# Moving an on-chip tile from a 32-byte offset to a multiple of 128 bytes

## The chip, the cores and the metric

The kernel runs on one core of a Trainium2 chip. The metric is the device time of one execution in microseconds; the median of the runs shown is compared.

## The reference

Two layers of a decoder trunk on 256 tokens of width 1024, all in float32. Each layer is a half-step feed-forward block, a token mixer and a second half-step feed-forward block, each on an RMS-normalised input. What matters here is the product of that normalised input with wide weight matrices:

```python
for l in range(DEPTH):
    h = h + 0.5 * swiglu(rms_norm(h, ffn1_norm[l]), ffn1_w_in[l], ffn1_w_out[l])
    u = rms_norm(h, mix_norm[l])
    (z_s, xbc, dt_s, qkv, z_d, b_d, a_d, gate_s, gate_d) = jnp.split(u @ w_in[l], split_points, axis=-1)
    y_s = mamba2_branch(z_s, xbc, dt_s, ...)      # state-space branch
    y_d = deltanet_branch(qkv, z_d, b_d, a_d, ...)  # gated delta rule branch
    merged = (jax.nn.sigmoid(gate_s) * (y_s @ ssm_w_branch[l])
              + jax.nn.sigmoid(gate_d) * (y_d @ dn_w_branch[l]))
    h = h + merged @ w_out[l]
    h = h + 0.5 * swiglu(rms_norm(h, ffn2_norm[l]), ffn2_w_in[l], ffn2_w_out[l])
return rms_norm(h, final_norm)
```

swiglu(x) is (silu(gate) * up) @ w_out with gate and up from x @ w_in (1024 to 2 x 2816).

## The kernel before

The weights stream from HBM in halves of 512 KB, in the order in which they are used: tile `wraw` takes a half, ScalarE rounds it to `whi`, VectorE writes the rest to `wlo` (lines 93 to 104). Every product of two float32 matrices is three matmuls of rounded parts: high by high, high by low, low by high. Five raw and five split halves are in flight.

`norm_in` makes the input of each sub-layer: per token tile of 128 tokens the norm, four transposes a half (`hnT`, in PSUM), then ScalarE writes the high part into `uTh` and VectorE the low part into `uTl`. Both are [128 partitions, 8 k tiles, 256 tokens], 8192 bytes a partition. They are read in two ways:

- `tok_chunk` (products named `t` and `f`) loads a 128 x 128 piece of uTh or uTl into TensorE and streams 512 columns of the weights past it (lines 209 to 211).
- `chan_chunk` (products named `fc`, `kk`, `qq`, `vv`, `zd`, `bc`, `xs`) loads a 128 x 128 piece of the weights and streams 256 columns, the tokens, of uTh or uTl past it (lines 214 to 216). `psm` does the same with 48 weight columns.

The products `o` (the second feed-forward matrix and the mixer's output) and `b` (the branches) have the form of `t`, but load the tiles gh, gl, mh, ml, bh or bl, which other pools hold.

In a feed-forward block `f` comes first, then 20 chunks of `fc`, then `o`. In the mixer the steps of the table ORDER follow each other: projections, the triangular inverse, the recurrence, the state-space products (`stb`, `ydb`, `yob`, which wait for the decay mask `dc`), gates and branches. The order on each engine is that in which the code issues its instructions, with the norm chains moved up by a priority.

Tiles of a pool with one buffer lie one behind the other in each partition, in the order of their first use, each padded to 32 bytes. In the pool `cpool` the order is h, cs, mhalf, one, Y0, Y1, uTh, uTl, nw, lp, rp, wsh, wsl; the pools of the weights and of everything else follow. `mhalf` is a column of 4 bytes, the exponent of the power that POOL takes for each norm. `lp` holds the parameters of the convolutions (LPW = 257 columns), `nw` the norm's weights, Y0 and Y1 are scratch of the inverse.

Of the kernel before, what the change touches and what calls it, by code (L numbers as in the profile page):

```python
# [7 lines left out]
F32 = mybir.dt.float32  # L8
# [8 lines left out]
P = 128  # L17
# [12 lines left out]
NRAW = 5  # L30
NSPL = 5
START = 2
# Steps of the token mixer in issue order; the weight stream follows it (see _layout).
# s decay scalars, M decay masks, z/k/q/v/d/b/x projections (gate of group, delta rule k q v and gate,
# state-space B C and x), K/Q/V what follows a projection, I triangular inverse, R recurrence,
# P state-space products of B and C, D decay, S/T state-space output, g branch gates,
# o/y first operand of the branches, N delta rule branch.
ORDER = """
z20 s z10 z11 s z21 s M k1 k0 q1 k2 k3 K1 K0 q3 q0 K3 K2 v0 q2 I Q0 I Q3 I z30 v1 z31 Q2 v2 V0 I v3
V1 I V3 I Q1 V2 d0 R R R b3 R b2 b0 R b1 R d2 R x00 R d1 x01 R d3 R R P R g100 g101 D0 S0 x10 T0 D1  # L40
# [5 lines left out]
def trunk_kernel(ctx, tc, x, wst, wsm, norms, lpar, rpar, cst, out):  # L46
# [38 lines left out]
    def small(shape, name, bufs=2):  # L85
        return sm.tile(shape, F32, tag=name, name=name, bufs=bufs)

# [1 line left out]
    n_halves = 2 * wst.shape[0]  # L89
    state = {"loaded": 0, "prepped": 0, "taken": 0, "last": None, "hold": False}  # L90
    raws, halves = {}, {}
# [32 lines left out]
            nc.sync.dma_start(nw[:], norms[i].partition_broadcast(P))  # L124
        return [nw[:, n * 512 : (n + 1) * 512] for n in range(2)]

# [1 line left out]
    h = cpool.tile([P, 2, D], F32, name="h")  # L128
    cs = cpool.tile([P, CW], F32, name="cs")
    row = slots.tile([1, D], F32, tag="y0", name="row")  # L130
# [14 lines left out]
    LIMT = cs[:, 3 * P + 64 : 4 * P]  # L145
    SEL = [cs[:, 4 * P : 5 * P], cs[:, 5 * P : 6 * P]]
    LAST = cs[:, 6 * P : 7 * P]
    mhalf = cpool.tile([P, 1], F32, name="mhalf")
    V.memset(mhalf[:], -0.5)

    one = cpool.tile([1, P], F32, name="one")
# [9 lines left out]
    uTl = cpool.tile([P, KT, S], F32R, name="uTl")  # L161

    def rstd_of(t):
        """1 / sqrt(mean(h^2) + eps) of one token tile"""
        ss = small([P, 2], "ss")
        for n in range(2):
            junk = tmp2("junk")
            act(junk[:], h[:, t, n * 512 : (n + 1) * 512], AF.Square, scale=1.0 / 32.0, accum_out=ss[:, n : n + 1])
        z = small([P, 2], "zz")
        ts(z[:, 0:1], ss[:, 0:1], ss[:, 1:2], ALU.add, EPS, ALU.add)  # L170
        rsqrt(z[:, 1:2], z[:, 0:1], [P, 1])
        return z[:, 1:2]
# [16 lines left out]
        return ins, done  # L189

    def norm_in(nw, add=None):
        """residual update (add) and the normalised, transposed, split input of the next sub-layer"""
        for t in range(2):
            with tc.high_priority(offset=PRI):
                if add:
                    add(t)
                ins, done = rms_chain(t, nw)
            if t == 0:
                state["hold"] = False
                n = state["taken"]  # L200
                if not add:
                    ahead("prepped", n + 1, prep)
                    with tc.issue_after(done[0].ins), tc.issue_after(done[1].ins):
                        ahead("prepped", n + START, prep)
                with tc.issue_after(ins.ins):
                    ahead("prepped", n + 2, prep)
# [9 lines left out]
        PE.matmul(ps, wl, mh, start=False, stop=stop)  # L216

    def tok_chunk(ps, ks):
        """512 output columns for both token tiles, contracted over the k tiles ks, two to a half"""
        ws = [(k, take()) for k in ks[::2]]  # L220
        for t in range(2):
            for k0, (wh, wl) in ws:
                for k in range(2):
                    kt = k0 + k
                    mm3(
                        ps[t][:],
                        uTh[:, kt, t * P : (t + 1) * P],
                        uTl[:, kt, t * P : (t + 1) * P],
                        wh[:, k * 512 : (k + 1) * 512],
                        wl[:, k * 512 : (k + 1) * 512],  # L230
                        kt == 0,
                        kt == KT - 1,
                    )

    def chan_chunk(ps):
        """256 output channels, channel-major: two halves of four k tiles."""
        ws = [take(), take()]
        for a in range(2):
            for q in range(2):
                wh, wl = ws[q]  # L240
                for k in range(4):
                    kt = 4 * q + k
                    c0 = k * 256 + a * P
                    mm3w(
                        ps[:, a * 256 : (a + 1) * 256],
                        wh[:, c0 : c0 + P],
                        wl[:, c0 : c0 + P],
                        uTh[:, kt, :],
                        uTl[:, kt, :],
                        kt == 0,  # L250
                        kt == KT - 1,
                    )

    def out_chunks(ps, stat, ks, last, group=1, split=False):
        """[k tile, 1024] halves accumulated in ps[t][n]; stat(kt, t) -> (hi, lo)."""
        for g0 in range(0, len(ks), group):
            kk = ks[g0 : g0 + group]
            ws = [(k, take()) for k in kk]
            for t in range(2):
                order = [(k, n) for n in range(2) for k in range(len(kk))]  # L260
                if t == 1 and not split:
                    order = [(k, n) for k in range(len(kk)) for n in range(2)]
                for k, n in order:
                    k, (wh, wl) = ws[k]
                    sh, sl = stat(k, t)
                    mm3(
                        ps[t][n][:], sh, sl,
                        wh[:, n * 512 : (n + 1) * 512], wl[:, n * 512 : (n + 1) * 512],
                        k == 0, k == last,
                    )  # L270

    def close(po, stat, n_k, nw):
        """last weights token tile by token tile, then the residual and the next norm"""
        out_chunks(po, stat, list(range(2)), n_k - 1, group=2)
        out_chunks(po, stat, list(range(2, n_k - NSPL)), n_k - 1)
        state["hold"] = True
        out_chunks(po, stat, list(range(n_k - NSPL, n_k)), n_k - 1, group=NSPL, split=nw is None)

        def add(t):
            for n in range(2):  # L280
                hv = h[:, t, n * 512 : (n + 1) * 512]
                stt(hv, po[t][n][:], 0.5, hv, ALU.mult, ALU.add)

        if nw is None:
            return add
        norm_in(nw, add)

# [1 line left out]
    def ffn(nxt):  # L289
        gh = [slots.tile([P, 8, S], F32R, tag=t_, name="gh") for t_ in ("sA", "sB", "sC")]  # L290
        gl = [slots.tile([P, 8, S], F32R, tag=t_, name="gl") for t_ in ("sD", "sE", "sF")]
# [34 lines left out]

        return close(po, stat, 22, nxt)

# [1 line left out]
    def mixer(l, nxt):  # L330
        with tc.issue_after(state["last"].ins):
            lp = cpool.tile([P, LPW], F32, tag="lp", name="lp")
            nc.sync.dma_start(lp[:], lpar[l])
            rp = cpool.tile([P, RPW], F32, tag="rp", name="rp")
            nc.sync.dma_start(rp[:], rpar[l].partition_broadcast(P))
            wsr = s2.tile([P, KT, 48], F32, tag="s2", name="wsr")
            nc.sync.dma_start(wsr[:], wsm[l])
# [11 lines left out]
        open_ = {}  # L349

        def tok_unit(key, part, done):
            """part 0 or 1 of the contraction, or all of it at once"""
            if part != 1:
                open_[key] = [accb("t0"), accb("t1")]
            tok_chunk(open_[key], range(KT) if part is None else range(4 * part, 4 * part + 4))
# [7 lines left out]
            tok_unit(("z", g), part, lambda t, ps: act(yz[g][:, t, :], ps[:], AF.Silu))  # L363

        def conv(ps, ti, dest, bias):
            """causal depthwise convolution and SiLU of one channel tile"""
            cp = lp[:, 5 * ti : 5 * ti + 5]
            ca = s2.tile([P, S], F32, tag="ca", name="ca", bufs=2)
            if bias:
# [6 lines left out]

        z_unit(0, None)

# [1 line left out]
        la = small([P, 2, 40], "la", 1)  # L380
        sp = small([P, 2, 40], "sp", 1)
        ac = small([P, 2, 40], "ac", 1)
# [59 lines left out]
        Gp = pq[:, 0]  # L442
        Bp = pq[:, 1]

# [1 line left out]
        kP = slots.tile([P, 4, 4, 2, 64], F32, tag="sA", name="kP")  # L446
        qP = slots.tile([P, 4, 4, 2, 64], F32, tag="sB", name="qP")
        Q = slots.tile([P, 16, P], F32, tag="sC", name="Q")
# [17 lines left out]
        oe = small([P, 4, 4], "oe", 1)  # L466

        def masks():
            """masked decay factors of all pairs, natural (dN) and transposed (dT)"""
            for hp in range(4):  # L470
                gb = s2.tile([P, 2, 4, 64], F32, tag="s2", name="gb")
                nc.sync.dma_start(
# [25 lines left out]
            act(eG[:], Gp, AF.Exp)  # L498

        def turned(src, hp):  # L500
            """token-major copy (in PSUM) and its squared norms"""
            bank = trb("turned")
            for c in range(4):
                PE.transpose(bank[:, c * P : (c + 1) * P], src[:, hp, c].rearrange("p a i -> p (a i)"), ident)
# [5 lines left out]
            return bank, nb  # L510

        def own(bank, x, y, hp):
            """x^T y of each head with itself, chunk by chunk"""
            for c in range(4):
                for a in range(2):
                    PE.matmul(
# [69 lines left out]
            return rest()  # L586

        def invert():
            """(I + Q)^-1: 16-blocks by substitution, one block to a partition, then doubling"""
            dq1 = dram.tile([P, 16, 16], F32, tag="dq1", name="dq1")  # L590
            dq2 = dram.tile([P, 2, 16, 16], F32, tag="dq2", name="dq2")
            for b in range(8):
# [151 lines left out]
            for _ in g:  # L744
                pass

# [1 line left out]
        def zd_unit(hp):  # L748
            ps = accb("zd")
            chan_chunk(ps)  # L750
# [138 lines left out]
            v = tg[s_][:, :, n * 512 : (n + 1) * 512]  # L889
            tok_unit(("g", s_, n), part, lambda t, ps: act(v[:, t, :], ps[:], AF.Tanh, scale=0.5))  # L890

# [1 line left out]
        brT = {}  # L893

        def dn_T(hp):
# [149 lines left out]
def _layout(inp):  # L1045
# [2 lines left out]
    f32 = np.float32  # L1048

    def cols(w):  # L1050
        """[K, 512*n] -> token-major units [128, 4 k tiles, 512], two per 512 columns"""
        n = w.shape[1] // 512
        a = w.reshape(2, 4, P, n, 512)
        return a.transpose(3, 0, 2, 1, 4).reshape(2 * n, P, 2048)

    def chans(w):
        """[1024, 256*n] -> channel-major units [128, 8 k tiles, 256]"""
        n = w.shape[1] // 256
        return w.reshape(8, P, n, 256).transpose(2, 1, 0, 3).reshape(n, P, 2048)

    def rows(w):
        """[256*n, 1024] -> units [128, 2 k tiles, 1024]"""
        n = w.shape[0] // 256
        return w.reshape(n, 2, P, 1024).transpose(0, 2, 1, 3).reshape(n, P, 2048)

# [96 lines left out]
```

## Time and profile before

| | |
|---|---|
| median of 3 runs | 1604.63 us (1603.78 to 1605.13) |
| profiled execution, first to last instruction | 1604.1 us; it lists no time of its own beside this span |
| granted TensorE clock | 0.997 |
| TensorE busy | 1581.0 us, 99% |
| VectorE busy | 1069.5 us, 67% |
| ScalarE busy | 885.3 us, 55% |
| HBM read | 280.94 MB |

A row of a group ends with its count, then its busy time and the mean of one in ns, then idle time before it. PE rows are matmuls, PEld rows the loading of the operand that stays in the array, which overlaps. A row of the timeline begins with the start and the duration in us. A row of the windows view begins with the stretch and its length, then busy time and count of PE, PEld, DVE, ACT and POOL (only those that have any), and ends with the granted clock, the share of the DMA engines and GB/s.

### The profile page before, as it was taken

To read this page: it belongs to the slowest core of one execution; us is meant where nothing else is said; L and a number is where in the kernel's file an instruction comes from. 1 tells how busy PE (TensorE), PEld (TensorE's weight loads), DVE (VectorE), ACT (ScalarE), POOL (GpSimd) and SP (SyncE) were. 2 spreads that over 40 slices of the span, in tenths; PEclk is the share of its full clock that TensorE was granted. 3 is DMA by queue.
4 is the path that set the end of the run, shared out by engine and by line. 5 is a ranking of instruction groups with operands and counts; after the bars stand their busy time and mean duration, and the time that the engine had idled before them with its cause. 6 is when DMAs were issued, how large, how long until landed. Compare 5 with 4: busy or idle time off the path is not lost.

```text
span 1604.1 us, 28895 instructions
## 1 busy us (share of the span) xinstructions
PE 1581.0 (99%) x11696; PEld 1425.3 (89%) x11696; DVE 1069.5 (67%) x1546; ACT 885.3 (55%) x1418; POOL 66.5 (4%) x60
## 2 busy tenths in 40 slices
PE   8999999999999999999999999999999999999998
PEld 7999879999888888999899987899998888889986
DVE  5555568957899666555465555699578986665554
ACT  5454467765575554444454445676756665454443
POOL 0000020000010000000000002010000100000000
PEclk9999999999999999999999999999999999999999
DMA  7555565543555455555465665556345455555562
GB/s 267 192 188 193 164 207 177 184 140 119 185 197 170 147 169 191 190 185 192 163 211 189 191 196 181 174 186 185 111 139 191 171 173 168 172 171 186 190 200 95
DMA packets 91915, 284.73 MB, mean 178 GB/s; under 512 B 22069, under 2 KB 23045, under 8 KB 90758
## 3 DMA queue, kind: packets, MB, share of 16 engines
q1 hardware_dynamic: 91782, 282.90, 54.2%
q8 instruction: 91, 1.49, 0.4%
q14 instruction: 42, 0.34, 0.1%
HBM read 280.94 MB, written 1.92 MB: 176 GB/s over the span
## 4 chain that ended last, share of the span: by engine, by line
PE 89%; DVE 4%; DMA 2%; ACT 2%; POOL 1%; issue 1%; SPq 0%; POOLq 0%; ACTq 0%; DVEq 0%
PE fc L214 9%; PE fc L216 9%; PE fc L215 9%; PE o L211 6%; PE o L210 5%; PE o L209 5%; PE t L209 3%; PE t L210 3%; PE t L211 3%; PE b L209 3%; PE b L210 3%; PE b L211 3%; PE xs L216 1%; PE xs L215 1%; PE xs L214 1%; DMA dc<-rdram 1%
## 5 line engine op out<-in xcount | busy, mean ns | idle before, releaser
L63 DVE TENSOR_TENSOR wlo<-wraw,whi 128x1024 fp32r<-128x1024 f32 x504 | 613.7, 1224 | 382.2 <-ACT whi L60 374.9
L60 ACT ACTIVATE whi<-wraw 128x1024 fp32r<-128x1024 f32 x504 | 531.1, 1060 | 424.6 <-PE fc L215 176.2
L214 PE MATMUL fc<-uTh,whi 128*128 128x256 f32 x1280 | 357.4, 279 | 0.0
L215 PE MATMUL fc<-uTl,whi 128*128 128x256 f32 x1280 | 357.0, 279 | 0.0
L216 PE MATMUL fc<-uTh,wlo 128*128 128x256 f32 x1280 | 357.0, 279 | 0.0
L215 PEld LDWEIGHTS fc<-uTl,whi 128*128 128x128 f32 x1280 | 240.6, 188 | 0.2
L214 PEld LDWEIGHTS fc<-uTh,whi 128*128 128x128 f32 x1280 | 240.6, 188 | 0.2
L216 PEld LDWEIGHTS fc<-uTh,wlo 128*128 128x128 f32 x1280 | 240.6, 188 | 0.0
L209 PE MATMUL o<-whi,gh 128*128 128x512 f32 x352 | 137.3, 390 | 0.0
L210 PE MATMUL o<-wlo,gh 128*128 128x512 f32 x352 | 137.2, 390 | 0.0
L211 PE MATMUL o<-whi,gl 128*128 128x512 f32 x352 | 137.0, 389 | 0.0
L209 PE MATMUL t<-whi,uTh 128*128 128x512 f32 x256 | 103.3, 404 | 1.2 <-ACT uTh L60 1.2
L210 PE MATMUL t<-wlo,uTh 128*128 128x512 f32 x256 | 101.6, 397 | 0.0
L211 PE MATMUL t<-whi,uTl 128*128 128x512 f32 x256 | 101.1, 396 | 0.0
L209 PE MATMUL b<-whi,bh 128*128 128x512 f32 x192 | 77.2, 404 | 3.7 <-ACT bh L60 3.7
L211 PEld LDWEIGHTS o<-whi,gl 128*128 128x128 f32 x352 | 66.1, 188 | 13.6
L210 PEld LDWEIGHTS o<-wlo,gh 128*128 128x128 f32 x352 | 66.1, 188 | 13.5
L209 PEld LDWEIGHTS o<-whi,gh 128*128 128x128 f32 x352 | 66.1, 188 | 13.5
L210 PE MATMUL b<-wlo,bh 128*128 128x512 f32 x192 | 75.9, 395 | 0.0
L211 PE MATMUL b<-whi,bl 128*128 128x512 f32 x192 | 74.9, 399 | 0.0
L214 PE MATMUL xs<-uTh,whi 128*128 128x256 f32 x256 | 73.1, 286 | 0.0
L216 PE MATMUL xs<-uTh,wlo 128*128 128x256 f32 x256 | 71.8, 280 | 0.4 <-DVE wlo L63 0.4
(262 smaller groups left out, 2940.4 us busy)
## 6 DMA issues: line engine op xcount, KB each, us to landing
wraw<-in_wst_dram SPq DMA_DIRECT2D x504, 512.0 KB, 4.4
dc<-rdram SPq DMA_DIRECT2D x8, 1024.0 KB, 8.1
nw<-in_norms_dram SPq DMA_DIRECT2D x6, 512.0 KB, 5.8
gb<-rdram SPq DMA_DIRECT2D x8, 256.0 KB, 6.1
h<-in_x_dram SPq DMA_DIRECT2D x4, 256.0 KB, 3.2
out_dram<-fo SPq DMA_DIRECT2D x4, 256.0 KB, 2.3
dq<-X SPq DMA_DIRECT2D x2, 256.0 KB, 4.7
cs<-in_cst_dram SPq DMA_DIRECT2D x1, 384.0 KB, 9.2
```

Of the source, the lines that this page charges most:

```text
L60: return A.activation(out=o, in_=i, func=func, **kw)
L63: return V.tensor_tensor(out=o, in0=a, in1=b, op=op)
L209: PE.matmul(ps, lh, rh, start=start, stop=False)
L210: PE.matmul(ps, lh, rl, start=False, stop=False)
L211: PE.matmul(ps, ll, rh, start=False, stop=stop)
L214: PE.matmul(ps, wh, mh, start=start, stop=False)
L215: PE.matmul(ps, wh, ml, start=False, stop=False)
L216: PE.matmul(ps, wl, mh, start=False, stop=stop)
```

## The change

`mhalf` is taken from the pool `sm`, at the far end of the partition, in place of `cpool`. With it gone, the tiles between it and rp move down by 32 bytes, and `lp` is declared 272 columns wide in place of 257, so that rp and everything behind it stay where they were. The transfer into lp still fills 257 columns. Comments are dropped, with empty lines in their place.

```diff
-    mhalf = cpool.tile([P, 1], F32, name="mhalf")
+    mhalf = sm.tile([P, 1], F32, name="mhalf", bufs=1)
...
-            lp = cpool.tile([P, LPW], F32, tag="lp", name="lp")
-            nc.sync.dma_start(lp[:], lpar[l])
+            lp = cpool.tile([P, 272], F32, tag="lp", name="lp")
+            nc.sync.dma_start(lp[:, 0:LPW], lpar[l])
```

No instruction is added, removed or moved on any engine. What changes is the start of these tiles within a partition (bytes, and the remainder by 128):

| tile | before | after |
|---|---|---|
| mhalf | 28288 (0) | 223872 (0) |
| one | 28320 (32) | 28288 (0) |
| Y0, Y1 | 28832, 30880 (32) | 28800, 30848 (0) |
| uTh | 32928 (32) | 32896 (0) |
| uTl | 41120 (32) | 41088 (0) |
| nw | 49312 (32) | 49280 (0) |
| lp | 53408 (32) | 53376 (0) |
| small tiles of `sm` (scalars, sums, la, sp, ac and others) | from 223872 on | each 32 further |

rp starts at 54464 (64) and wsh at 54912 (0) in both; the weight tiles, gh, gl, mh, ml, bh and bl start on multiples of 128 in both.

## The prediction

> **What bounds the kernel now.** I read the head of the page first, then the chain, then the groups of TensorE instructions, and then the times at which single matmuls start.
>
> ```profile
> span 1604.1 us, 28895 instructions
> PE 1581.0 (99%) x11696; PEld 1425.3 (89%) x11696; DVE 1069.5 (67%) x1546; ACT 885.3 (55%) x1418; POOL 66.5 (4%) x60
> PE 89%; DVE 4%; DMA 2%; ACT 2%; POOL 1%; issue 1%; SPq 0%; POOLq 0%; ACTq 0%; DVEq 0%
> ```
>
> TensorE is busy 99% of the span and holds 89% of the chain that ended last. So a matmul that becomes shorter counts nearly in full, and the question is only whether the addresses change a matmul. The groups give the counts by kind (lines 214 to 216 have the same count each, as have 209 to 211):
>
> ```profile
> L214 PE MATMUL fc<-uTh,whi 128*128 128x256 f32 x1280 | 357.4, 279 | 0.0
> L209 PE MATMUL o<-whi,gh 128*128 128x512 f32 x352 | 137.3, 390 | 0.0
> L209 PE MATMUL t<-whi,uTh 128*128 128x512 f32 x256 | 103.3, 404 | 1.2 <-ACT uTh L60 1.2
> L214 PE MATMUL xs<-uTh,whi 128*128 128x256 f32 x256 | 73.1, 286 | 0.0
> L214 PE MATMUL kk<-uTh,whi 128*128 128x256 f32 x128 | 35.9, 281 | 0.0
> L209 PE MATMUL f<-whi,uTh 128*128 128x512 f32 x64 | 26.4, 415 | 0.9 <-ACT uTh L60 0.9
> ```
>
> The first operand named is the one that streams, the second the one that is loaded. In the channel-major products (fc, xs, and kk, qq, vv, zd, bc with 128 a line each) uTh and uTl stream, 256 columns at a time: 3 x (1280 + 256 + 5 x 128) = 6528 matmuls. In the token-major ones (t, f) uTh and uTl are loaded and the weights stream, 512 columns: 3 x (256 + 64) = 960. The o products have the same form as t, but load gh and gl, which already start on a multiple of 128 bytes.
>
> The durations in these rows overlap (390 ns x 1056 is far more than the time that o takes), so they price nothing. I take the distance between starts instead: first and last row of an unbroken run in the timeline, and the count from a windows row cut to that tile.
>
> ```profile
> 31.34 0.28 PE L215 MATMUL fc<-uTl,whi 128*128 128x256 f32 x1
> 137.51 0.28 PE L216 MATMUL fc<-uTh,wlo 128*128 128x256 f32 x1
> 31.34:137.51 106.17, 106.17 (x912) 106.17 (x911) 7.87 (x19) 6.96 (x19) 1.00 0.59 190
> 137.63 0.39 PE L209 MATMUL o<-whi,gh 128*128 128x512 f32 x1
> 193.19 0.39 PE L211 MATMUL o<-whi,gl 128*128 128x512 f32 x1
> 137.62:193.20 55.58, 55.57 (x246) 46.00 (x246) 1.38 (x2) 0.00 (x0) 1.00 0.57 182
> 518.33 0.39 PE L210 MATMUL t<-wlo,uTh 128*128 128x512 f32 x1
> 534.66 0.39 PE L211 MATMUL t<-whi,uTl 128*128 128x512 f32 x1
> 518.32:534.67 16.35, 16.35 (x72) 13.15 (x70) 0.60 (x1) 1.00 0.51 165
> 217.32 0.28 PE L214 MATMUL psm<-uTh,wsh 128*48 128x256 f32 x1
> 219.99 0.28 PE L216 MATMUL psm<-uTh,wsl 128*48 128x256 f32 x1
> 217.31:220.00 2.69, 2.68 (x24) 2.68 (x23) 0.00 (x0) 1.00 1.03 337
> ```
>
> In the fc and t windows one of the counted matmuls began before the window. So fc: 106.17 us / 910 intervals = 116.67 ns. o: 55.56 / 245 = 226.8 ns. t: 16.33 / 70 = 233.3 ns. psm (uT streams, only 48 columns are loaded): 2.67 / 23 = 116 ns. The clock column reads 1.00 in all of them.
>
> This is the row that decides the sign. t and o stream the same weights tiles in the same 512 columns at the same clock; t loads from an address with remainder 32, o from one with remainder 0, and t takes 6.5 ns more for each matmul.
>
> **The change part by part.**
>
> *The loaded operand (t, f).* After the change uTh and uTl have remainder 0 as gh and gl have. I take the o spacing: 960 x 6.5 ns = 6.2 us. Nothing in the rows makes it a loss.
>
> *The streamed operand (6528 matmuls).* Before shows no 256-column stream from an aligned tile, so this is bounded. If a matmul costs a fixed part, not below zero, and a part per column, then 256 aligned columns cost at least half of 512 aligned ones: 226.8 / 2 = 113.4 ns, a gain of 3.3 ns. If only the loaded operand feels its address, they stay at 116.7: nothing. If the grid works the other way on a stream, by as much for each column as on the load (6.5 ns on 512 columns, so 3.3 on 256), they go to 120 ns, a loss of 3.3 ns. I take 113.4, because of a match: half of t's 233.3 is 116.67, exactly the fc spacing. Every matmul with one operand off the grid passes 2.19 columns per ns, whichever operand it is and however long the stream, and the only kind with both on the grid passes 2.26. psm says the same from another side: with 48 loaded columns in place of 128 the spacing stays at 116, so it is not the load's length that holds fc. So 6528 x 3.3 = 21.5 us. psm adds 48 x 3 ns = 0.1 us.
>
> By the Trainium skill, "TensorE: Matmul & The Clock Gate", section "Part 2: What happens when you issue a matmul", loading the next weights takes no read bandwidth from the running matmul, since there are two read ports. By that rule the address of a loaded operand could not lengthen a matmul that streams 512 columns; the 6.5 ns between t and o speak against it, and the sum by it would lose its first term.
>
> *What ScalarE and VectorE do with the moved tiles.*
>
> ```profile
> L60 ACT ACTIVATE uTh<-hnT 128x512 fp32r<-128x512 f32 x24 | 14.0, 595 | 12.8 <-PE hnT L184 11.6
> L60 ACT ACTIVATE tg<-t 128x512 f32<-128x512 f32 x16 | 9.5, 593 | 9.5 <-PE t L211 9.2
> L63 DVE TENSOR_TENSOR uTl<-hnT,uTh 128x512 fp32r<-128x512 f32 x24 | 15.7, 687 | 5.8 <-ACT uTh L60 5.7
> L63 DVE TENSOR_TENSOR ml<-mT,mh 128x512 fp32r<-128x512 f32 x8 | 5.5, 688 | 0.1
> ```
>
> Writes to the tiles that are off the grid take as long as those to tg and ml, which are on it. I cost nw, lp, Y0, Y1, one and the small tiles (which move by 32 bytes the other way) at nothing by the same rows. The wider lp moves no more data: its transfer still fills 257 columns. mhalf is read by POOL as before. One loaded operand goes off the grid, la, which eight matmuls (psr) load: 8 x 6.5 ns, 0.05 us.
>
> *What of the gain lies off the path.* In the mixer the chain leaves TensorE for a stretch:
>
> ```profile
> 407.49 1.22 DVE wlo L63
> 409.11 8.53 DMA dc<-rdram
> 428.39 2.29 DVE dc L63
> 437.22 1.10 PE stb L853 x2
> 407.00:485.00 78.00, 75.05 (x592) 65.30 (x589) 71.01 (x97) 50.51 (x74) 8.99 (x3) 0.98 0.56 192
> 407.00:485.00 78.00, 49.81 (x224) 36.53 (x224) 0.00 (x0) 0.00 (x0) 0.98 0.56 192
> 407.00:485.00 78.00, 35.05 (x112) 21.06 (x112) 0.00 (x0) 0.98 0.56 192
> ```
>
> The four chain rows show stb waiting for a mask that comes by DMA and VectorE; the window rows (all work, then uTh's, then uTl's instructions) show VectorE busy 71.0 of 78 us (third pair) and 224 + 112 = 336 of the matmuls in question. Five projections and two half gates stand there: 240 matmuls of 256 columns, 96 t. If they shrink, TensorE waits longer at stb and for the weight splits behind it. I give all of it up, in both layers: 480 x 3.3 + 192 x 6.5 = 2.8 us.
>
> At each of six norms the first token tile's matmuls cover the second tile's norm:
>
> ```profile
> 199.19 0.39 PE L209 MATMUL t<-whi,uTh 128*128 128x512 f32 x1
> 203.85 0.40 PE L211 MATMUL t<-whi,uTl 128*128 128x512 f32 x1
> 204.35 0.66 PE L184 MATMUL hnT<-cs,hn 128*128 128x128 f32 x4
> ```
>
> About 22 matmuls finish before the transposes hnT can begin, which wait on VectorE. Their gain becomes wait: 6 x 22 x 6.5 ns = 0.9 us.
>
> Sum: 6.2 + 21.5 + 0.1 - 2.8 - 0.9 = 24.1 us. The profiled span is 1604.1 us, 0.5 below the median of the runs, 1604.63; taken from the median it gives 1580.5 us.
>
> **The rivals.**
>
> *Only the loaded operand gains* (streams stay at 116.7). For it: the equal 116.67 may be the pace of something else that happens once a matmul. Against it: the match with t, and psm. Then 960 - 192 - 132 = 636 matmuls x 6.5 = 4.1 us: 1600.5.
>
> *Between the two*: streams at 114 to 116; 1584 to 1597.
>
> *Streams gain more than half of o.* The rows hold a pace for loading alone:
>
> ```profile
> 239.80 0.39 PE L494 MATMUL lb<-ac,cs 128*128 128x32 f32 x2
> 240.02 0.37 PE L214 MATMUL kk<-uTh,whi 128*128 128x256 f32 x1
> ```
>
> Two lb matmuls load 128 columns each and stream 32; they take 0.22 us, 110 ns each. At 110 the 6048 streams on the path would save 6.7 ns each: 40.5 + 4.1, so 1560. It needs most of o's 226.8 ns to be a cost that 256 columns do not bear.
>
> *Slower: two reads on one grid collide.* If a stream and a load whose remainders are equal meet in one bank, fc, whose operands are now 32 bytes apart, would go to the 120 ns of the bound above: 6528 x 3.3 = 21.5 us more, less 4.1 for the loads: 1622. It decides from 117.3 ns up (4.1 us / 6528 = 0.6 ns). Against it: t, whose operands are 32 bytes apart too, is slower than o, whose are not.
>
> *Nothing happens.* If t is slower than o for its loop (24 matmuls into one bank in a row, where o changes bank more often) and not for its address, all stays: 1604.6. In o three matmuls in a row go to one bank without a slow one among them, so I give it little. The Trainium skill, "SBUF — State Buffer", section "Door 1: The DMA port swizzle (why [64,N] ≈ [32,N])", has lines of 16 bytes, within which reads are at full pace; 32 is a multiple of 16, so by that rule the offset could not matter. The 6.5 ns are against it, if they are the address's.
>
> **How the numbers follow.** Streams at about 113.4: 0.47. Between: 0.08. Loaded operand alone: 0.27. Streams below 113: 0.07. Nothing: 0.06. Slower: 0.05. About 0.2% (3.2 us) is what a measurement of this kernel can tell from no change. The loaded operand alone lies just above it, so 0.08 of its 0.27 go to "same": faster 0.47 + 0.08 + 0.07 + 0.19 = 0.81, same 0.08 + 0.06 = 0.14, slower 0.05. The likeliest case alone lies between 1575 and 1586 (0.7 ns either way on the streams). The range goes from 1573 to 1602: it takes in the first three cases, 0.82.
>
> **What would show it.** fc starts 113.4 ns apart, t 226.8, both as constant as o now. The o and b spacings, uTh's 595 and uTl's 687 ns stay. The waits at stb and hnT grow by 0.3 to 1 us each. I am wrong if fc stays at 116.7 (then the match with t was chance), if t stays at 233, or if the streams shrink and VectorE or the weight transfers (190 GB/s in the fc row) take the time back.

## The result: 14 us slower

The changed kernel takes 1618.91 us (median of 4 runs) against 1604.88 us for the one before; the ratio is 1.0083, with a 95% interval from 1.007 to 1.0095. The forecast was 1580.5 us, with a range from 1573 to 1602.

The head of the page of the changed kernel, with the same three lines as were shown of before:

```profile
span 1616.5 us, 28895 instructions
PE 1593.8 (99%) x11696; PEld 1443.6 (89%) x11696; DVE 1069.8 (66%) x1546; ACT 885.7 (55%) x1418; POOL 66.1 (4%) x60
PE 89%; DVE 4%; DMA 2%; ACT 2%; POOL 1%; issue 1%; SPq 0%; POOLq 0%; ACTq 0%; DVEq 0%
```

The span grew by 12.4 us and TensorE's busy time by 12.8. VectorE and ScalarE work as long as before, and the chain has the same shares. So the matmuls themselves changed. The starts of the same four runs of matmuls, from the timeline and from a windows row cut to the tile:

```profile
31.04 0.28 PE L215 MATMUL fc<-uTl,whi 128*128 128x256 f32 x1
140.24 0.28 PE L216 MATMUL fc<-uTh,wlo 128*128 128x256 f32 x1
31.04:140.24 109.20, 109.20 (x911) 109.20 (x911) 7.86 (x19) 6.93 (x19) 1.00 0.57 186
140.36 0.40 PE L209 MATMUL o<-whi,gh 128*128 128x512 f32 x1
195.92 0.39 PE L211 MATMUL o<-whi,gl 128*128 128x512 f32 x1
523.70 0.40 PE L210 MATMUL t<-wlo,uTh 128*128 128x512 f32 x1
539.60 0.39 PE L211 MATMUL t<-whi,uTl 128*128 128x512 f32 x1
221.31:223.96 2.65, 2.63 (x24) 2.63 (x23) 0.00 (x0) 1.00 0.91 330
```

The fc run has 910 intervals in 109.20 us: 120.0 ns, where it had 116.67. The o run has 245 in 55.56 us: 226.8, unchanged. The t run has 70 in 15.90 us: 227.1, where it had 233.3. The 24 psm matmuls, which load only 48 columns, begin 114 ns apart, where they had 116. The clock column reads 1.00.

The lengthening can be read in two groups as well, a stream and the load of its weights, before (first two rows) and after:

```profile
L214 PE MATMUL fc<-uTh,whi 128*128 128x256 f32 x1280 | 357.4, 279 | 0.0
L214 PEld LDWEIGHTS fc<-uTh,whi 128*128 128x128 f32 x1280 | 240.6, 188 | 0.2
L214 PE MATMUL fc<-uTh,whi 128*128 128x256 f32 x1280 | 362.5, 283 | 0.0
L214 PEld LDWEIGHTS fc<-uTh,whi 128*128 128x128 f32 x1280 | 245.7, 192 | 0.2
```

Both are 4 ns longer. Averaged over all intervals within a chunk, from the starts in the trace: fc went from 116.68 to 119.98 ns (3840 matmuls), the other 256-column streams from 116.82 to 119.86 (2688), t and f from 233.14 to 227.68 (960). That makes 12.7 + 8.2 - 5.2 = 15.7 us; 14.0 were measured. Each of the four runs of fc puts the changed kernel about 3.1 us further behind. In the mixer a part comes back: the matmul that starts at 407.53 us before is 6.3 us late after, the one at 575.02 us only 4.8. Which wait takes this up was not separated; TensorE's waits at stb and hnT are almost the same in both (2.2 and 2.0 us, 4.7 and 5.3).

### The profile page after: what moved, and what is told of

Read it like the earlier page. It is cut to its first block, busy times and chain, and to the rows that moved or that the text cites. A ratio compares the mean times of both kernels' runs of the same rounds, so it can differ in the third digit from the quotient of the medians.

```text
span 1616.5 us, 28895 instructions
## 1 busy us (share of the span) xinstructions
PE 1593.8 (99%) x11696; PEld 1443.6 (89%) x11696; DVE 1069.8 (66%) x1546; ACT 885.7 (55%) x1418; POOL 66.1 (4%) x60
## 4 chain that ended last, share of the span: by engine, by line
PE 89%; DVE 4%; DMA 2%; ACT 2%; POOL 1%; issue 1%; SPq 0%; POOLq 0%; ACTq 0%; DVEq 0%
PE fc L216 10%; PE fc L214 10%; PE fc L215 9%; PE o L211 6%; PE o L209 5%; PE o L210 5%; PE t L209 3%; PE t L210 3%; PE t L211 3%; PE b L209 3%; PE b L211 2%; PE b L210 2%; PE xs L215 1%; PE xs L214 1%; PE xs L216 1%; DMA dc<-rdram 1%
## 5 line engine op out<-in xcount | busy, mean ns | idle before, releaser
L214 PE MATMUL fc<-uTh,whi 128*128 128x256 f32 x1280 | 362.5, 283 | 0.0
L216 PE MATMUL fc<-uTh,wlo 128*128 128x256 f32 x1280 | 362.2, 283 | 0.0
L215 PE MATMUL fc<-uTl,whi 128*128 128x256 f32 x1280 | 362.2, 283 | 0.0
L215 PEld LDWEIGHTS fc<-uTl,whi 128*128 128x128 f32 x1280 | 245.7, 192 | 0.2
L214 PEld LDWEIGHTS fc<-uTh,whi 128*128 128x128 f32 x1280 | 245.7, 192 | 0.2
L216 PEld LDWEIGHTS fc<-uTh,wlo 128*128 128x128 f32 x1280 | 245.7, 192 | 0.0
```

Of the source, the lines that this page charges most:

```text
L214: PE.matmul(ps, wh, mh, start=start, stop=False)
L215: PE.matmul(ps, wh, ml, start=False, stop=False)
```

## The experiments

The theories. (1) What counts is the difference between the address of the stream and the address of the load, by its remainder; equal remainders are the slow case for a 256-column stream. (2) The stream's own address counts, whatever is loaded. (3) The length of the load counts: two reads collide only where the load lasts as long as the stream. Experiments on one core are compared with the kernel before on the same chip (medians 1604.9 to 1605.1 us).

### The matmuls alone

A kernel of matmuls only, in blocks of 96 (256 columns) or 48 (512), all in one PSUM bank each, over four tiles that lie whole multiples of 256 bytes apart. The streamed part begins s bytes and the loaded part l bytes above a multiple of 256 from the start of its tile, written "s on l" below. The products and their order by lines are those of mm3w and mm3.

```diff
+    def chan(name, s, l, cols=128, n=96):
...
+        ps = accp.tile([P, 512], F32, tag="acc", name=name)
+        for i in range(n):
+            kt = (i // 3) % 8
+            c0, s0 = kt * 256 + l // 4, kt * 256 + s // 4
+            lo = wl if i % 3 == 2 else wh
+            st = ul if i % 3 == 1 else uh
+            PE.matmul(ps[0:cols, 0:256], lo[:, c0 : c0 + cols], st[:, s0 : s0 + 256], start=i == 0, stop=i == n - 1)
...
```

> Leaves the whole trunk out: 45 blocks of matmuls on their own, each of the form of chan_chunk (128 loaded columns, 256 streamed) or tok_chunk (512 streamed), with the start of the streamed and of the loaded operand set apart in bytes. If what counts is the difference between the two remainders (theory 1), equal remainders of 0, 32, 64 and 96 all give 120 ns from start to start, and a stream 32 off gives 116.7. If the stream's own address counts (theory 2), 0 on 0 gives 120 and 32 on 32 gives 116.7. If the length of the load counts (theory 3), 48 and 64 loaded columns give 113 to 114 at equal remainders and 112 and 128 give 120. The 512-column blocks repeat 226.7 with the load at 0 and 233.3 with the load at 32.

First and last matmul of three blocks, from the timeline of this kernel: pae has s = 32 on l = 0, paj 112 on 0, pas 32 on 32.

```profile
64.30 0.28 PE L72 MATMUL pae<-uh,wh 128*128 128x256 f32 x1
75.39 0.28 PE L72 MATMUL pae<-uh,wl 128*128 128x256 f32 x1
121.21 0.28 PE L72 MATMUL paj<-uh,wh 128*128 128x256 f32 x1
131.98 0.28 PE L72 MATMUL paj<-uh,wl 128*128 128x256 f32 x1
222.81 0.28 PE L72 MATMUL pas<-uh,wh 128*128 128x256 f32 x1
234.21 0.28 PE L72 MATMUL pas<-uh,wl 128*128 128x256 f32 x1
```

With 95 intervals each: 116.7, 113.4 and 120.0 ns. No VectorE instruction and no weight transfer runs beside them, and only the first few matmuls of a block overlap ScalarE's one read of the block before (0.4 us). So the paces of the trunk come about with TensorE and its two reads alone. All blocks of this probe (48) and the second (49) that load 128 columns and stream 256 (mean of the last two thirds of each, from the starts; two numbers where a pair was tried more than once and differed):

| streams of 256, 128 loaded | ns |
|---|---|
| 0 on 0, 32 on 32, 64 on 64, 96 on 96 | 120.0 each |
| 16 on 0 | 116.7 |
| 32 on 0 | 116.7, 117.8 |
| 64 on 0, 192 on 0 | 113.3 or 117.8, 117.8 |
| 80 on 0, 96 on 0 | 120.0, 120.1 |
| 112 on 0, 368 on 0 | 113.3 each time |
| 240 on 0, 256 on 0 | 117.2, 120.0 |
| 4, 8, 24, 100, 104, 108, 116, 120, 124 on 0 | 119.8 to 123.3 |
| 40, 48, 128 on 0 | 119.1, 118.3, 118.7 |
| 0 on 16, 32, 48, 64 | 118.3, 118.3, 117.8, 113.3 or 117.8 |
| 0 on 80, 96, 112, 128 | 118.7, 120.0, 119.9, 118.6 |
| 64 on 32, 32 on 64, 32 on 48, 48 on 64 | 116.7, 118.3, 118.3, 117.2 |

Four equal pairs at 120 speak for theory 1 and against theory 2 (which had 116.7 for 32 on 32). In the pairs tried, the pattern repeats with 256 bytes and not with 128: 112 and 368 agree, and so do 0 and 256, while 240 differs from 112, and 128 from 0. Pairs at the same distance by 256 agree to about 1 ns, or show the same two paces: 64 on 32 with 32 on 0, 32 on 64 with 0 on 32, 0 on 64 with 192 on 0 (117.8, once 113.3), 32 on 48 with 48 on 64 (118.3, 117.2). It is no rule of the form "on the grid or off it": 112 is the fastest of all, 113.3, and 96 is as slow as 0.

### uT at 64, at 96, and everything at 32

Three versions of the whole kernel. The first two widen the tiles ahead of uTh by 64 or 96 bytes and put the rest back in step behind lp; the third starts from the kernel before and widens lp, so that the weights and all behind them move to remainder 32, where uTh and uTl already are.

```diff
# u64 (u96: P + 24 and 312)
-    one = cpool.tile([1, P], F32, name="one")
+    one = cpool.tile([1, P + 16], F32, name="one")
...
-            lp = cpool.tile([P, 272], F32, tag="lp", name="lp")
+            lp = cpool.tile([P, 320], F32, tag="lp", name="lp")
# w32, from the kernel before
-            lp = cpool.tile([P, LPW], F32, tag="lp", name="lp")
+            lp = cpool.tile([P, 265], F32, tag="lp", name="lp")
...
```

> uTh and uTl stay at remainder 32 as before, but the weights and everything behind them go to 32 as well, so the operands are on equal remainders again, off the grid. Theory 1 (difference): fc 120, t 226.7, time 1619. Theory 2 (the stream's own address): fc 116.7, t 233 (its load is at 32), and o and b, which now load from 32, go to 233 as well: 1605 plus 1824 x 6.5 ns, 1617. The two differ in fc and t, not in the time.

w32 took 1619.01 us, ratio 1.0086 (1.007 to 1.0101). Its fc run:

```profile
31.08 0.28 PE L215 MATMUL fc<-uTl,whi 128*128 128x256 f32 x1
140.26 0.28 PE L216 MATMUL fc<-uTh,wlo 128*128 128x256 f32 x1
```

That is 910 intervals in 109.18 us, 120.0 ns, and t came to 227.7: the changed kernel again, to the tenth of a per cent, with no operand of these products on a multiple of 128. In the kernel too it is the difference that counts, and theory 2 falls. o, both of whose operands moved, kept its 227.0 ns.

> uTh and uTl at remainder 96, the weights at 0. If steps of 64 bytes set the pace, this is the kernel before again: fc 116.7, t 233, time 1605. If the whole 128 bytes count, fc differs from both 116.7 and 120.

u96 took 1623.5 us, ratio 1.0113 (1.0096 to 1.013): fc 120.0, t 234.2, slower than the changed kernel because t loses as well.

> uTh and uTl at remainder 64, the weights at 0. Theory 1 and theory 2 both take fc off the 120 ns of equal remainders: 113.3 to 116.7, and t to 227 to 233; the time is 1580 to 1608. If only the remainder 32 is better than 0, fc stays at 120 and the time at 1619.

u64 took 1606.59 us, ratio 1.001 (0.9996 to 1.0024), with ten runs between 1602.4 and 1612.1. Its four feed-forward blocks run the same code at the same distance by 256, and the trace has fc at 117.8 ns in the first and third and at 113.3 in the second and fourth. So one distance can hold more than one rhythm. None of the theories had said so.

### Is a pace the offset's own

> Leaves the whole trunk out: 47 blocks of matmuls on their own, as in the first probe, now to see whether a pace belongs to an offset or to the way into it. If the difference (stream minus load) alone sets the pace, 112 against 0 gives 113.3 ns each of the four times it is tried, and so do 0 against 16, 32 against 48 and 48 against 64 (also 16 behind); 0 against 0 gives 120 and 16 or 32 against 0 116.7 each time; in the 512-column blocks loads at 16, 32 against 16 and 112 against 96 give 226.7. If the way into the rhythm counts as well, the same pair gives different paces at different places of the list. If the length of the load counts, 64 loaded columns at 0 against 0 stay at 113.3 and 120 and 128 are at 120.

The first probe had 64 on 0 (pag) at 117.8; this is 64 on 0 (pav) in the second, with its tiles laid out in the same way, then 64 loaded columns (pbb) and 120 (pbg: 128 loaded), both at 0 on 0:

```profile
255.57 0.28 PE L72 MATMUL pav<-uh,wh 128*128 128x256 f32 x1
266.34 0.28 PE L72 MATMUL pav<-uh,wl 128*128 128x256 f32 x1
322.03 0.28 PE L72 MATMUL pbb<-uh,wh 128*64 128x256 f32 x1
332.80 0.28 PE L72 MATMUL pbb<-uh,wl 128*64 128x256 f32 x1
377.54 0.28 PE L72 MATMUL pbg<-uh,wh 128*128 128x256 f32 x1
388.94 0.28 PE L72 MATMUL pbg<-uh,wl 128*128 128x256 f32 x1
```

113.4, 113.4 and 120.0 ns. At equal remainders the length of the load decides: 32, 48, 64 and 80 loaded columns gave 113.3, 96 gave 116.1, 112 and 120 gave 117.8, 128 gave 120.0 (in the first probe 48 columns were at 117.3 and not at 113.3). Off equal remainders a shorter load does not help: 64 columns at 32 on 0 took 119.1, at 64 on 0 116.7, at 112 on 0 116.7. So theory 3 holds at equal remainders alone. 112 on 0 reached 113.3 in every trial, at times after up to 12 matmuls of 114 to 122. Its fellows 0 on 16, 32 on 48 and 48 on 64, which have the same remainder by 128, gave 118.3, 118.3 and 117.2: by 256 they lie at 240, and 240 on 0 had 117.2. In the 512-column blocks, 0 on 16 was at 226.7 in the first probe and at 233.3 twice in this one: another pair with two rhythms. 112 on 0, the steady one of the 256-column streams, is at 226.7 in this probe and at 231 in the third.

### uT at 112, at 16, and back at 32

From the changed kernel, both tiles get 64 columns more and are used from an offset; the weights stay on multiples of 128.

```diff
-    uTh = cpool.tile([P, KT, S], F32R, name="uTh")
+    uTh = cpool.tile([P, KT * S + 64], F32R, name="uTh")[:, 28:28 + KT * S].rearrange("p (k s) -> p k s", k=KT)
```

and the same for uTl (28 columns are 112 bytes; u16 has 4, u32 has 8, u240 has 60).

> uTh and uTl at remainder 112, the weights at 0. From the first probe: fc and the other 256-column streams 113.3 ns, t 233.3 as before. If the probe holds in the kernel: 1605 - 6528 x 3.3 ns + about 1.6 lost behind other waits = 1585. If the kernel falls into another rhythm than the probe: fc 117.8 to 120 and 1606 to 1620.

u112 took 1589.54 us, ratio 0.9897 (0.988 to 0.9913): 16 us faster than the kernel before and 29 faster than the changed one.

```profile
span 1587.5 us, 28895 instructions
PE 1561.8 (98%) x11696; PEld 1405.1 (89%) x11696; DVE 1069.1 (67%) x1546; ACT 884.7 (56%) x1418; POOL 66.4 (4%) x60
31.23 0.28 PE L215 MATMUL fc<-uTl,whi 128*128 128x256 f32 x1
134.41 0.28 PE L216 MATMUL fc<-uTh,wlo 128*128 128x256 f32 x1
L214 PE MATMUL fc<-uTh,whi 128*128 128x256 f32 x1280 | 352.5, 275 | 0.0
```

fc: 910 intervals in 103.18 us, 113.4 ns. Over all chunks fc has 113.46 and the other streams 114.06, since a chunk after a pause often needs some 15 matmuls of 113 to 122 ns to fall into step; t stays at 233.4. The sum of 3840 x 3.22 and 2688 x 2.76 ns is 19.8 us, and TensorE's busy time fell by 19.2. The span fell by 16.6, so about 2.6 us of it became waits; the median of the runs fell by 15.5, 4.5 less than expected.

> uTh and uTl at remainder 16, the weights at 0. From the first probe: fc 116.7 as before, t 226.7. If both hold: 1605 - 4.1 = 1601, the rival of the prediction in which the loaded operand alone gains.

u16 took 1604.89 us, ratio 0.9998 (0.9985 to 1.001), not 1601. fc was at 116.7 as expected; t was at 233.3 in some chunks and at 226.7 in others, 229.8 in the mean, and the chunks of the other streams at 113.3 to 119.2, 117.5 in the mean. By these paces t and f gained 3.2 us and the other streams lost 1.7; what is left, 1.5 us, is too small for the interval to show.

> The change, but with uTh and uTl put back to remainder 32; everything else stays where the change put it (mhalf, one, Y0, Y1, nw, lp). If uTh and uTl alone made the difference: fc 116.7, t 233.3 and 1605. If another moved tile had a part in it, the time lies between 1606 and 1618.

u32 took 1605.35 us, ratio 1.0001 (0.9991 to 1.0012), with fc at 116.67 and t at 233.15. With uTh and uTl put back, the change is undone: the other moved tiles have no part in it.

### The difference again, and the period

> The weights and what lies behind them at remainder 32, uTh and uTl at 144: the difference of u112 (112) with other addresses. If the difference sets the pace: fc 113.3, t 233.3, 1589.5 as u112. If the addresses themselves do: fc between 116.7 and 120 and 1604 to 1619.

This is w32 with uTh and uTl 112 bytes above it (the same edit as u112). It took 1587.76 us, ratio 0.9897 (0.9872 to 0.9922), with fc at 113.45 and t at 233.44: u112 again at other addresses.

> uTh and uTl at remainder 112 as in u112, but 128 bytes further on (240 above a multiple of 256 of the weights' start). If the remainder by 128 is all that counts: fc 113.3 and 1589.5 as u112. If the pattern has a period of 256, as the second probe has it (240 against 0: 117.2): fc 117.2 and 1605 to 1608.

u240 took 1604.6 us, ratio 0.9999 (0.9985 to 1.0014).

```profile
32.14 0.28 PE L215 MATMUL fc<-uTl,whi 128*128 128x256 f32 x1
138.74 0.28 PE L216 MATMUL fc<-uTh,wlo 128*128 128x256 f32 x1
```

910 intervals in 106.60 us: 117.1 ns. 128 bytes more cost all of u112's gain, so the period is more than 128, as in the probes. t came to 228.1 there, nearly as in the changed kernel, though its load begins 112 bytes above a multiple of 128.

### Which load a stream meets

> Leaves the whole trunk out: 30 blocks of matmuls on their own. In the alternating blocks, even and odd matmuls have offsets of their own, so that a stream and its own load are equal while the stream and the load of the next matmul differ, or the other way round. If a stream meets the load of the matmul behind it: with streams 0, 112 and loads 112, 0 each stream equals the next load and the block takes 120 ns; with streams 0, 112 and loads 0, 112 it differs from it and takes another pace. If it meets its own load: the other way round. The blocks of equal offsets repeat 120 (0 on 0), 113.3 (112 on 0) and 116.7 to 117.8 (32 on 0).

Streams 0, 112 with loads 0, 112 (each stream equal to its own load) took 120.0 and 120.1 ns; streams 0, 112 with loads 112, 0 (each equal to the load of the next matmul) 118.3 both times. With 64 in place of 112 it was 116.7 and 120.1, with 32 118.9 and 118.3, with 16 117.8 and 118.9. The two orders differ, but not by one rule: this leaves open which load a stream collides with.

## Why the prediction was wrong

The step that failed is the second term of the sum, the streamed operand: 256-column streams were to go from 116.7 to 113.4 ns and went to 120.0, so that -21.5 us became +20.9 (12.7 + 8.2).

It rested on two inferences. The first was that t is slow because its load is "off the grid", so that each operand has a grid of its own; the runs show a difference between two addresses (w32 and w32u144 reproduce two other kernels at shifted addresses). The sign of a difference matters as well (64 on 32 took 116.7 and 32 on 64 118.3): fc was 32 above its load, t's stream 32 below, and nothing about the one follows from the other. The second was the match of fc with half of t. That was chance: after the change half of t is 113.6 and fc is at 120.0, and in the probes the two move apart, a 512-column block being at 233.3 for loads at 32, 48, 64, 112 and 128, where the 256-column blocks range from 113.3 to 120. The bound of 113.4 itself was sound: no block of 256-column streams kept a pace below 113.3, and u112 reaches it. Equal remainders are only not the way to it.

The first term, the loaded operand, held in its size: 6.5 ns were forecast, t went from 233.3 to 227.1 in the run shown, and over all chunks the gain was 5.2 us of 6.2. Its reason did not hold: in w32 t is at 227.7 with the load at remainder 32. The 512-column blocks of the first probe have 226.7 for 0 on 0, 32 on 32 and 64 on 64, so it is the equal remainders that made t as fast as o, not a load on a multiple of 128. The changes costed at nothing cost nothing that the interval could show (u32). The stretch at stb was rightly kept out of the sum. It began with the split wlo at 407.49 and reached stb at 437.22 before; here are its ends and the mask's DMA after, then in u112:

```profile
413.81 1.24 DVE wlo L63
415.44 8.86 DMA dc<-rdram
443.89 1.10 PE stb L853 x2
403.36 1.22 DVE wlo L63
404.97 9.18 DMA dc<-rdram
433.74 1.10 PE stb L853 x2
```

29.7 us became 30.1 and, in u112, 30.4. Both differences are those of the DMA, which took 8.53 us before. The 336 matmuls of the prediction are those of the whole window of 78 us; in this stretch stand 96 streams and 48 t. After the change these nearly cancel, 0.3 us more and 0.3 less, so u112 is the better witness: there t is unchanged, the streams need some 0.2 us less, and the stretch is no shorter.

The rival on the other side, two reads on equal remainders that collide, had the pace to the nanosecond (120) and the time, 1622, about 3 us from 1618.91. A part of that was luck: its 120 was 116.7 with the same 3.3 ns put on the other side, and equal remainders are not the only slow ones (80 and 96 on 0 are at 120 too). I gave it 0.05, with the argument that t, 32 apart too, is slower than o. That argument took 32 above and 32 below for the same thing, and 512 columns for twice 256. I also read psm as a sign that the length of the load does not matter, since with 48 loaded columns it kept fc's pace. At equal remainders the length does matter, 113.3 ns for 64 columns and 120.0 for 128. And psm was a poor witness: its loads lie 192 bytes apart from one k tile to the next, so its distance changes within the run, and its starts were 113 to 121 ns apart where nearly all of fc's were 116 or 117.

The rule of the Trainium skill on two read ports ("TensorE: Matmul & The Clock Gate", "Part 2: What happens when you issue a matmul") is not borne out by these float32r matmuls: the distance of the two operands moves the pace of the stream between 113.3 and 123.3 ns, and at equal remainders the length of the load moves it between 113.3 and 120.0. Nor do lines of 16 bytes ("SBUF — State Buffer", "Door 1: The DMA port swizzle (why [64,N] ≈ [32,N])") tell the paces: 16, 80, 96 and 112 on 0 are whole lines apart and take 116.7, 120.0, 120.1 and 113.3.

## What to carry to other kernels

A matmul streams one tile while another is loaded, and the distance between the two addresses can set the pace; so measure a few offsets in a kernel of matmuls alone (one run gave 48) before a layout is chosen, and do not take round addresses for good ones. A slow pair in one kind of matmul need not be slow in another kind in which the roles are exchanged or the stream has another length. Prefer an offset that came out the same in every trial and in the whole kernel, as 112 did here for the 256-column streams.

## What the runs showed of the hardware

- Float32r matmuls of 128 loaded and 256 streamed columns run at 113.3 to 123.3 ns, and 512-column ones at 226.7 to 236.7, at a granted clock of 1.00 and with almost nothing else running. In the pairs tried, the distance between the streamed and the loaded address, by 256 bytes, told which paces came up.
- The same distance can hold two steady rhythms: 117.8 and 113.3 ns in feed-forward blocks of one execution (u64), and in the same form of block, 64 on 0, of the first and second probe.
- At the start of the first probe the equal pair took 213 ns for some 27 matmuls before it came to 120. The clock column reads 1.00 there too, so the profile does not say why, and no other pair stands in such a stretch:

```profile
17.09 0.41 PE L72 MATMUL paa<-ul,wh 128*128 128x256 f32 x1
19.22 0.41 PE L72 MATMUL paa<-uh,wl 128*128 128x256 f32 x1
```

Ten intervals in 2.13 us. What in the memory collides, and why 112 settles at once or after 15 matmuls, stays open.
